# The causal convolution of a hybrid encoder layer as products with diagonal matrices, with v by token, a shorter reciprocal root and two x blocks transposed by TensorE

## The chip, the cores and the metric

One core of a Trainium2 chip runs the whole layer in one program. The metric is the time on the device in microseconds, lower is better. For the kernel before there are three timed runs and one profiled execution.

## The reference, cut to what matters

Two requests (x_prompt and x_sample, 2048 tokens of 1024 features each, in float32) go through one encoder layer with the same weights. The change concerns group B, the gated DeltaNet branch.

```python
def encoder_layer(x, mem, ...):
    hx = rms_norm(x, pre_g)
    proj = hx @ w_in
    a_u, a_z, b_qkv, b_z, b_gates, c_qkv, c_z, d_q, d_z = jnp.split(proj, IN_SPLITS, axis=-1)
    y_a = fourier_mix(a_u, w_fnet) * jax.nn.silu(a_z)
    y_b = gdn_branch(b_qkv, b_gates, conv_w, ...) * jax.nn.silu(b_z)
    ...
    out = jnp.concatenate([y_a, y_b, y_c, y_d], axis=-1) @ w_out
    return x + rms_norm(out, post_g)

def gdn_branch(qkv, gates, conv_w, ...):
    act = jax.nn.silu(centred_dwconv(qkv, conv_w)).astype(jnp.float32)
    q, k, v = jnp.split(act, 3, axis=-1)
    q = l2_norm(q.reshape(b, l, h, HEAD_DIM)) * (HEAD_DIM ** -0.5)
    k = l2_norm(k.reshape(b, l, h, HEAD_DIM))
    ...
    o_f = gdn_chunked(q, k, v, g[:, :, 0], beta[:, :, 0])
    o_b = rev(gdn_chunked(rev(q), rev(k), rev(v), ...))
```

centred_dwconv is a convolution over five tokens of each of 768 channels by itself (256 of q, k and v, in 4 heads of 64); gdn_chunked works in chunks of 64 tokens, each of which first needs k, q and v of its tokens, then an inverse of a triangular matrix, and then the state of the chunk before.

## The kernel before, in words

Numbers of float32 precision are made from f16 products: each operand is split into a high and a low f16 half, and a product is three products (lines 484 to 486 with token blocks as the right operand, 494 to 496 with them as the left, 500 to 502 elsewhere). A scheduler orders the instructions of each engine once, at build time, by priorities of the parts ("bands") and its own estimates; on the chip each engine then runs its list in that order. So an instruction that waits holds up all behind it on its engine, and a transfer is issued when its queue (SP's, or ACT's for stores of projections) comes to it.

The program, in the order of its data:

- pass_a, for each request 8 blocks of 256 tokens. xblock (lines 448 to 470) normalises a block, splits it (ACT L466 high, DVE L213 low) and lets SP's DMA transpose it (L468) to features by tokens; block() stores it for later sweeps (xTd). For each block the units k, q, v and ag (a_u and the gates) are projected on TensorE (feat, pj, L484 to L486), evacuated by ACT (L561) into st, and stored by ACT's queue into braw, in HBM, f32, with two tokens of padding at either end (L518, L519). For the very first block the weights of each unit are loaded and split just ahead (L385, L415, L419, L421; L431 takes the maxima that set a scale).
- The convolution, conv_pair (L880 on), for each block and each of k, q, v. It loads 260 tokens of two 128-channel groups from braw (craw, L885) and sums five taps by channel: ACT the first (L889), DVE the other four (L891, one instruction of 128x256 for each tap and group), then tanh on ACT (L893) and the product that makes the SiLU on DVE (L894). ACT and POOL split the result into f16 halves (L901, L227: kq for k and q, vt for v). v is then transposed by a DMA on SP (L960) from channels by tokens to tokens by channels, vr, and stored for the chain. Squares of k and q are summed over a head on PE (pss, L909), and norms() makes reciprocal roots of them.
- gdn_pair, for each two chunks: kbd on DVE, the products of k with k and q (PE L500 to L502 into p12, in the PSUM tags ga and gq in turn), and DVE's products with the decay mask (L1013). The last of these ends what is called the preparation here. gdn_sub (from L1056) inverts the triangular matrices, gdn_chain (L1133) runs the states in order, 32 steps each way for both requests.
- Beside and behind them, as fillers by priority: the Fourier part (fnet), memory and neighbourhood attention, the second sweep (pass_b, projections for the attention groups), the third (pass_z, gate paths) and the output projection (pass_o).

rsqrt (L232 to L245) computes a reciprocal root on DVE: a first guess by integer shift and subtraction (L239, L240), and three Newton steps of three instructions (L243 to L245).

## Time and profile before

| | us |
|---|---|
| median of three runs | 2527.11 (2523.99 to 2535.14) |
| the profiled execution | 2518.5 |
| its span | 2516.7 |
| busy in the span: PE, DVE, POOL, ACT | 2006.7, 2013.1, 1128.9, 1034.4 |
| first projection on PE starts | 64.4 |
| last evacuation of pass_a (L568) starts | 653.9 |
| last mask product of the preparation (L1013) starts | 892.9 |
| state chain (L1133), first and last start | 1485.8, 2111.7 |

The profile's times are of one execution; its span leaves out 1.8 us around it. PE is TensorE, PEld its weight loads (which run beside products), DVE VectorE, ACT ScalarE, POOL GpSimd, SP the engine that issues most transfers. Busy time is the union of the instructions of an engine. PEclk is the granted share of TensorE's full clock.

### The profile page before, as it was taken

Reading aid. Unit: us, or ns where it says so; the run is one execution under the profiler, and the core shown is the slowest. Engines: PE = TensorE matmul, PEld = TensorE weight load, DVE = VectorE, ACT = ScalarE, POOL = GpSimd, SP = SyncE. Lnnn points to the kernel's source line nnn. Section 1 sums busy time; section 2 is a strip of 40 time slices with the busy share of each in tenths; the row PEclk is TensorE's granted clock in tenths of the full one; section 3 lists DMA queues with packets and bytes.
Section 4 is the critical chain, followed back from the end, with each engine's and each line's share of the span. In section 5 each row is a group of like instructions: output and inputs, shape, how many; then the busy total and the mean of one; then the engine's idle time right before and its main releaser. Section 6 shows DMA issues by size and latency. Waiting matters only on the chain. (4 is left out here: it accounts for less than half of the span.)

```text
span 2516.7 us, 60042 instructions
## 1 busy us (share of the span) xinstructions
PE 2006.7 (80%) x23715; PEld 1701.4 (68%) x23715; DVE 2013.1 (80%) x4757; ACT 1034.4 (41%) x2434; POOL 1128.9 (45%) x1181
## 2 busy tenths in 40 slices
PE   0787778787446786899698988887788899899998
PEld 0665667665335675777576767777677788688887
DVE  3579988989999979668989667887679977677774
ACT  1455554553354421334056423554445523332322
POOL 1225655445476667535786152232234343533220
PEclk9988899998768988999799999999999999899999
DMA  9899899999635694599789877999999995555543
GB/s 94 193 210 178 200 232 239 233 209 234 180 94 159 168 222 118 142 218 179 153 187 200 181 195 210 229 199 210 198 214 224 217 279 164 169 182 187 187 161 118
DMA packets 827484, 476.08 MB, mean 189 GB/s; under 512 B 556864, under 2 KB 789952, under 8 KB 818752
## 3 DMA queue, kind: packets, MB, share of 16 engines
q1 hardware_dynamic: 802624, 438.67, 76.0%
q10 hardware_dynamic: 24576, 33.56, 4.5%
q8 instruction: 186, 3.05, 0.5%
q14 instruction: 98, 0.80, 0.1%
HBM read 243.38 MB, written 163.73 MB: 162 GB/s over the span
## 5 line engine op out<-in xcount | busy, mean ns | idle before, releaser
L484 PE MATMUL pj<-xT,w 128*128 128x256 f16 x2592 | 741.1, 286 | 119.7 <-DMA xT<-xh 35.7
L486 PE MATMUL pj<-xT,w 128*128 128x256 f16 x2592 | 739.5, 285 | 4.0 <-POOL w L421 4.0
L485 PE MATMUL pj<-xT,w 128*128 128x256 f16 x2592 | 740.6, 286 | 0.0
L485 PEld LDWEIGHTS <-w 128*128 128x128 f16 x2592 | 265.1, 102 | 109.4 <-issue 67.7
L484 PEld LDWEIGHTS <-w 128*128 128x128 f16 x2592 | 265.1, 102 | 102.7 <-issue 31.4
L486 PEld LDWEIGHTS <-w 128*128 128x128 f16 x2592 | 265.3, 102 | 52.8 <-POOL w L421 9.4
L502 PE MATMUL po<-w,oy 128*128 128x256 f16 x1024 | 280.3, 274 | 1.4 <-DVE oy L716 1.4
L500 PE MATMUL po<-w,oy 128*128 128x256 f16 x1024 | 280.7, 274 | 0.8 <-ACT oy L715 0.8
L501 PE MATMUL po<-w,oy 128*128 128x256 f16 x1024 | 280.9, 274 | 0.0
L891 DVE SCALAR_TENSOR_TENSOR cacc<-craw,cws,cacc 128x256 f32<-128x256 f32 x384 | 244.4, 671 | 7.4 <-ACT cacc L889 6.2
L494 PE MATMUL pj<-w,xT 128*128 128x272 f16 (+1 forms) x512 | 153.3, 300 | 43.8 <-ACT st L561 21.8
L230 POOL TENSOR_TENSOR oy<-oy,oz 128x512 f32<-128x512 f32 x60 | 101.0, 1704 | 187.7 <-ACT oy L701 179.4
L1165 POOL COPY bk<-rA 64x512 f16<-64x512 f16 x124 | 85.8, 692 | 208.9 <-PE pw L502 171.2
L765 ACT ACTIVATE oj<-po,wsc_o 128x256 f32<-128x256 f32 x128 | 59.5, 469 | 243.9 <-PE po L502 243.1
L495 PE MATMUL pj<-w,xT 128*128 128x272 f16 (+1 forms) x512 | 153.0, 299 | 0.8 <-POOL w L421 0.8
L496 PE MATMUL pj<-w,xT 128*128 128x272 f16 (+1 forms) x512 | 152.9, 299 | 0.0
L421 POOL TENSOR_TENSOR w<-wt,w 128x512 f16<-128x512 f32 (+1 forms) x70 | 85.1, 1223 | 145.9 <-ACT w L419 118.4
L227 POOL TENSOR_TENSOR mP<-mP,mP 128x1024 f16<-128x1024 f32 x32 | 71.6, 2241 | 137.0 <-DVE ty L1503 52.9
L500 PE MATMUL pno<-nPT,nv 128*128 128x64 f16 x704 | 78.5, 199 | 57.9 <-DMA nPT<-np__2819_27983 20.2
L1170 DVE COPY b<-rA 64x1536 f16<-64x1536 f16 x128 | 112.4, 878 | 8.1 <-DMA cT<-T 3.7
L227 POOL TENSOR_TENSOR km<-kt,km 128x256 f16<-128x256 f32 x128 | 96.4, 775 | 38.0 <-ACT km L1009 36.2
L1485 ACT ACTIVATE mP<-pms,ty,mds 128x256 f32<-128x256 f32 x128 | 71.0, 560 | 97.7 <-DVE ty L1482 76.0
(442 smaller groups left out, 6162.7 us busy)
## 6 DMA issues: line engine op xcount, KB each, us to landing
xT<-xTd SPq DMA_DIRECT2D x32, 1024.0 KB
rec<-km SPq DMA_DIRECT2D x32, 768.0 KB
rA<-rec SPq DMA_DIRECT2D x64, 384.0 KB
xTd<-xT SPq DMA_DIRECT2D x16, 1024.0 KB
sz<-st ACTq DMA_DIRECT2D x64, 256.0 KB
oz<-sz SPq DMA_DIRECT2D x16, 1024.0 KB
out_dram<-oo SPq DMA_DIRECT2D x32, 512.0 KB
craw<-braw SPq DMA_DIRECT2D x48, 260.0 KB
```

Source lines behind the costliest of these rows:

```text
L227: self.nc.gpsimd.tensor_tensor(out=out, in0=a, in1=b, op=ALU.subtract)
L484: nc.tensor.matmul(ps, whi, xhi, start=(kt == 0), stop=False)
L485: nc.tensor.matmul(ps, whi, xlo, start=False, stop=False)
L486: nc.tensor.matmul(ps, wlo, xhi, start=False, stop=(kt == KT - 1))
L494: nc.tensor.matmul(ps, xhi, whi, start=(kt == 0), stop=False)
L495: nc.tensor.matmul(ps, xhi, wlo, start=False, stop=False)
L496: nc.tensor.matmul(ps, xlo, whi, start=False, stop=(kt == KT - 1))
L500: nc.tensor.matmul(ps, whi, xhi, start=start, stop=False)
L501: nc.tensor.matmul(ps, whi, xlo, start=False, stop=False)
L502: nc.tensor.matmul(ps, wlo, xhi, start=False, stop=stop)
L891: nc.vector.scalar_tensor_tensor(out=acc[:, f], in0=raw[:, f, t:t + CB], scalar=w[:, t:t + 1], in1=acc[:, f], op0=ALU.mult, op1=ALU.add)
L1170: nc.vector.tensor_copy(b1[s, :, h].rearrange("p (d x) c -> p d x c", d=2), ra[s, :, 0:12])
```

## The change

- The convolution becomes products on TensorE. conv_diag makes, once, a table cdg of diagonal matrices 64x64 for each unit, channel group, head and tap, as f16 high and low halves (three pieces, each two DVE instructions and one of ACT over 1280 elements, and a small one for the scale). braw is kept as f16 high and low halves: ACT evacuates the high half, DVE's split_lo the low one (from PSUM, 128x512), and only then ACT's queue stores both. craw holds for one head the high half of 64 channels on partitions 0 to 63 and the low half on 64 to 127; four loads of 64 partitions bring it where there was one, and it has four buffers instead of two. Ten products (five taps, two table halves) add up in PSUM (pcv, in the tags ga and gq) for each group and head: 64 output rows by 256 columns for q and k (L935), with the two heads in turn. tanh and the SiLU product (now L939) read PSUM.
- v's products (L929) have the tokens as weights and the table as right operand, 64 by 64 each, with the two groups in turn, so they come out by token: vr is written at once, and the DMA transposes L960 go.
- The low half of q and v is now DVE's (split_lo, L214), k's stays with POOL. Scales move into the table and back by powers of two (CSH, cinp).
- rsqrt takes 8 instructions: one for the guess, one Newton step of three, and one step of higher order of four.
- xblock has a switch: the first two blocks of the first request are transposed by PE (64 transposes of 128x128) with eight ACT evacuations of 128x1024, in place of four DMA transposes.

```diff
     def rsqrt(self, x, out, eng=None):
...
-        nc.vector.tensor_scalar(out=y.bitcast(I32), in0=x.bitcast(I32), scalar1=1, scalar2=None, op0=ALU.logical_shift_right)
-        nc.vector.tensor_scalar(out=y.bitcast(I32), in0=y.bitcast(I32), scalar1=-1.0, scalar2=float(0x5F3759DF),
-                                op0=ALU.mult, op1=ALU.add)
-        for i in range(3):
-            eng.scalar_tensor_tensor(out=t, in0=y, scalar=-0.5, in1=y, op0=ALU.mult, op1=ALU.mult)
-            eng.scalar_tensor_tensor(out=t, in0=t, scalar=1.0, in1=x, op0=ALU.mult, op1=ALU.mult)
-            eng.scalar_tensor_tensor(out=(out if i == 2 else y), in0=t, scalar=1.5, in1=y, op0=ALU.add, op1=ALU.mult)
+        stt = lambda o, a, s, b, op: eng.scalar_tensor_tensor(out=o, in0=a, scalar=s, in1=b, op0=op, op1=ALU.mult)
+        nc.vector.tensor_scalar(out=y.bitcast(I32), in0=x.bitcast(I32), scalar1=-0.5, scalar2=float(0x5F3759DF), op0=ALU.mult, op1=ALU.add)
+        stt(t, y, -0.5, y, ALU.mult)
+        stt(t, t, 1.0, x, ALU.mult)
+        stt(y, t, 1.5, y, ALU.add)
...
+        c = math.sqrt(0.375)
+        stt(t, y, c, y, ALU.mult)
+        stt(t, t, 1.0, x, ALU.mult)
+        stt(t, t, -1.25 / c, t, ALU.add)
+        stt(out, t, 1.875, y, ALU.add)
...
-    def xblock(self, rows):
+    def xblock(self, rows, pe=False):
...
-            nc.sync.dma_start(dst[:, :, :, t * P:t * P + P].rearrange("p l k t -> p (l k) t"), hl.rearrange("p l c -> p (l c)"), transpose=True)
+            if pe:
+                for l in range(2):
+                    pt = self.pat.tile([P, KT, P], F16, name=self.nm("pxt"), tag=PSS[l])
+                    for k in range(KT):
+                        nc.tensor.transpose(pt[:, k], hl[:, l, k * P:k * P + P], self.ident16)
+                    nc.scalar.activation(dst[:, l, :, t * P:t * P + P], pt, AF.Copy)
+            else:
...
-            xT = self.xblock(x[tb * 256:tb * 256 + 256, :])
+            xT = self.xblock(x[tb * 256:tb * 256 + 256, :], pe=r == 0 and tb < 2)
...
-                nc.scalar.activation(st, ps, AF.Copy, scale=2.0 ** -19)
-                nc.scalar.dma_start(D[f"braw{r}"][:, f0:f0 + 2, 2 + tb * 256:258 + tb * 256], st)
+                st = self.stage([P, 2, 2, 256], F16)
+                nc.scalar.activation(st[:, :, 0], ps, AF.Copy, scale=2.0 ** -19)
+                self.split_lo(nc.vector, st[:, :, 1], ps, st[:, :, 0], 2.0 ** -19)
+                nc.scalar.dma_start(D[f"braw{r}"][:, f0:f0 + 2, :, 2 + tb * 256:258 + tb * 256], st)
...
+    def conv_diag(self, pp):
...
+        cg = self.cdg = pp.tile([P, 3, 20, 2, 64], F16, name="cdg", tag="cdg")
+        for i, u in ((1, "k"), (0, "q"), (2, "v")):
...
+            d = pp.tile([P, 20, 64], F32, name=self.nm("cdf"), tag="cdf")
+            nc.vector.tensor_tensor(out=d, in0=self.i2.unsqueeze(1).to_broadcast([P, 20, 64]), in1=w.unsqueeze(2).to_broadcast([P, 20, 64]), op=ALU.mult)
+            nc.scalar.activation(cg[:, i, :, 0], d, AF.Copy)
+            nc.vector.tensor_tensor(out=cg[:, i, :, 1], in0=d, in1=cg[:, i, :, 0], op=ALU.subtract)
...
     def conv_pair(self, r, pp, tb, u):
...
-        raw = pp.tile([P, 2, CB + 4], F32, name=self.nm("craw"), tag="craw", bufs=2)
-        nc.sync.dma_start(raw, self.D[f"braw{r}"][:, 2 * i:2 * i + 2, tb * CB:tb * CB + CB + 4])
...
-        for f in range(2):
-            w = self.cws[:, 2 * i + f]
-            nc.scalar.activation(acc[:, f], raw[:, f, 0:CB], AF.Copy, scale=w[:, 0:1])
-            for t in range(1, 5):
-                nc.vector.scalar_tensor_tensor(out=acc[:, f], in0=raw[:, f, t:t + CB], scalar=w[:, t:t + 1], in1=acc[:, f], op0=ALU.mult, op1=ALU.add)
...
-        nc.vector.scalar_tensor_tensor(out=acc, in0=e, scalar=1.0, in1=acc, op0=ALU.add, op1=ALU.mult)
+        raw = pp.tile([P, 2, 2, CB + 4], F16, name=self.nm("craw"), tag="craw", bufs=4)
+        src = self.D[f"braw{r}"].rearrange("(h e) a l t -> l h e a t", h=2)
+        for l in range(2):
+            for h in range(2):
+                nc.sync.dma_start(raw[64 * l:64 * l + 64, :, h], src[l, h, :, 2 * i:2 * i + 2, tb * CB:tb * CB + CB + 4])
+        pv = self.pgd.tile([P, 2 * CB], F32, name=self.nm("pcv"), tag="ga" if u == "q" else "gq")
+        dg = lambda f, h, t, l: self.cdg[:, i, (f * 2 + h) * 5 + t, l]
+        S = [(t, l) for t in range(5) for l in range(2)]
...
         if u == "v":
...
+            for n in range(CB // 64):
+                for h in range(2):
+                    for k, (t, l) in enumerate(S):
+                        for f in range(2):
+                            nc.tensor.matmul(pv[half(f), n * P + 64 * h:n * P + 64 * h + 64], raw[:, f, h, n * 64 + t:n * 64 + t + 64], dg(f, h, t, l),
+                                             start=(k == 0), stop=(k == 9))
         else:
+            for f in range(2):
+                for k, (t, l) in enumerate(S):
+                    for h in range(2):
+                        nc.tensor.matmul(pv[half(h), f * CB:f * CB + CB], dg(f, h, t, l), raw[:, f, h, t:t + CB], start=(k == 0), stop=(k == 9))
...
+        nc.scalar.activation(e, pv, AF.Tanh, scale=self.cinp[:, i:i + 1])
+        nc.vector.scalar_tensor_tensor(out=acc, in0=e, scalar=1.0, in1=pv, op0=ALU.add, op1=ALU.mult)
...
+            if u == "k":
+                self.gsub(dst[1], ac, dst[0])
+            else:
+                for f in range(2):
+                    self.split_lo(nc.vector, dst[1][:, f], ac[:, f], dst[0][:, f], sc)
...
-        self.nc.sync.dma_start(vr.rearrange("p n (x c) -> p (n x) c", c=P), self.vt.rearrange("p n l f c -> p (n l f c)"), transpose=True)
```

The order that the scheduler gives is another one throughout. Two places show it. The first is SP's list at the start, from the first padding stores of braw on (xt is a block of x on its way in, xT the transposed block, w the weights; w_277 and w_315 are q's, w_369 and w_408 v's). Before:

```order
L518 DMA braw_209<-ty_210 768x1x2
L519 DMA braw_209<-ty_210 768x1x2
L385 DMA w_277<-in_w_in_dram 128x8x256
L385 DMA w_369<-in_w_in_dram 128x8x64 x3
L456 DMA xt_654<-in_x_prompt_dram 128x1024
L518 DMA braw_3153<-ty_3154 768x1x2
L519 DMA braw_3153<-ty_3154 768x1x2
L468 DMA_TRANSPOSE xT_107<-xh_133 128x16x128
L468 DMA_TRANSPOSE xT_107<-xh_137 128x16x128
L385 DMA w_369<-in_w_in_dram 128x8x64
L385 DMA w_464<-in_w_in_dram 128x8x256
```

Now:

```order
L533 DMA braw_246<-ty_247 1536x1x2 x2
L392 DMA w_315<-in_w_in_dram 128x8x256
L392 DMA w_408<-in_w_in_dram 128x8x64 x3
L463 DMA xt_691<-in_x_prompt_dram 128x1024
L533 DMA braw_3219<-ty_3220 1536x1x2 x2
L463 DMA xt_695<-in_x_prompt_dram 128x1024
L463 DMA xt_1099<-in_x_prompt_dram 128x1024
L392 DMA w_408<-in_w_in_dram 128x8x64
L392 DMA w_504<-in_w_in_dram 128x8x256
```

The two transposes ahead of v's last piece of weights are gone, loads of x blocks stand there instead, and the padding is 1536 rows at a time.

The second is DVE's list in the middle of the convolution (gates, gw, gam, beta and ke belong to the gates of the chain, nrm to the norms, xh to the next x block). Before:

```order
L894 SCALAR_TENSOR_TENSOR cacc_13113<-cexp_13124,cacc_13113 128x512
L569 TENSOR_SCALAR gates_215<-pj_1461,wsc_ag 128x16
L213 SCALAR_TENSOR_TENSOR xh_1905<-xt_1881,ty_1890,xh_1905 128x1024
L213 SCALAR_TENSOR_TENSOR xh_1909<-xt_1885,ty_1890,xh_1909 128x1024
L891 SCALAR_TENSOR_TENSOR cacc_13283<-craw_13281,cws,cacc_13283 128x256 x2
L918 COPY nrm_13133<-pss_13042 64x8 x4
L891 SCALAR_TENSOR_TENSOR cacc_13283<-craw_13281,cws,cacc_13283 128x256
L569 TENSOR_SCALAR gates_215<-pj_1488,wsc_ag 128x16
```

Now:

```order
L214 SCALAR_TENSOR_TENSOR xh_2294<-xt_2273,ty_2278,xh_2294 128x1024
L224 TENSOR_TENSOR gw_1623<-gw_1623 128x32
L939 SCALAR_TENSOR_TENSOR cacc_13852<-cexp_13851,pcv_13810 128x512
L849 TENSOR_SCALAR beta_976<-gw_1619 128x4x8
L214 SCALAR_TENSOR_TENSOR st_1788<-pj_1739,st_1788 128x2x256
L858 COPY gam_979<-pga_1622 128x4x8
L865 TENSOR_SCALAR ke_978<-ke_978 128x4x8
L467 TENSOR_SCALAR ty_2413<-ty_2413 128x2
```

The runs of L891 are gone; between one L939 and the next stand the gates' work and a split of a projection, st, that was not there before.

## Rows read from the trace of the kernel before

**Rows 1.** Windows: stretch and length, busy us (instructions) by engine, then clock and DMA.
```profile
core 0: us, PE busy (x) PEld busy (x) DVE busy (x) ACT busy (x) POOL busy (x), PEclk, DMA share, GB/s
...
130.00:660.00 530.00, 410.82 (x3754) 341.05 (x3755) 485.90 (x1241) 251.50 (x556) 275.41 (x291) 0.88 0.99 218
660.00:890.00 230.00, 136.47 (x1259) 110.90 (x1257) 221.19 (x529) 107.42 (x243) 150.97 (x161) 0.77 0.53 142
890.00:1500.00 610.00, 511.55 (x5286) 414.20 (x5284) 495.61 (x898) 224.77 (x520) 353.28 (x369) 0.92 0.82 177
1500.00:2110.00 610.00, 507.81 (x9545) 452.91 (x9544) 482.34 (x1316) 281.99 (x709) 206.23 (x255) 0.96 0.94 217
2110.00:2517.00 407.00, 387.04 (x3488) 341.36 (x3486) 272.03 (x566) 127.29 (x334) 116.81 (x76) 0.98 0.48 168
0.00:890.00 890.00, 600.35 (x5403) 492.96 (x5404) 763.16 (x1978) 400.39 (x872) 452.62 (x481) 0.87 0.87 188
```

**Rows 2.** Line L1013: instructions, minimum/median/maximum ns, first and last start.
```profile
L1013 DVE TENSOR_TENSOR mt<-p,df x64: 401/414/419, 211.4 to 892.9; 128x256 f32<-128x256 f32 x64
```

**Rows 3.** Waits: who, for whom; us in total, times, longest.
```profile
ACT cexp L893 <- DVE cacc L891: 84.3, 27, 6.6
...
PE p L500 <- DVE mt L1013: 41.3, 25, 4.2
...
PE pj L484 <- DVE st L213: 32.6, 9, 6.7
...
ACT cacc L889 <- DMA craw<-braw: 16.8, 9, 3.5
```

**Rows 4.** Groups by form on DVE, the costliest: count, busy us, mean ns.
```profile
L891 DVE SCALAR_TENSOR_TENSOR cacc<-craw,cws,cacc 128x256 f32<-128x256 f32 x384 | 244.4, 671 | 7.4 <-ACT cacc L889 6.2
```

**Rows 5.** Groups by form on DVE: the reciprocal root's first step.
```profile
L243 DVE SCALAR_TENSOR_TENSOR ty<-ty 128x2 f32<-128x2 f32 x99 | 26.8, 271 | 2.4
```

**Rows 6.** Groups by form on DVE: the tanh product, a split from PSUM.
```profile
L894 DVE SCALAR_TENSOR_TENSOR cacc<-cexp,cacc 128x512 f32<-128x512 f32 x48 | 34.8, 724 | 2.2 <-ACT cexp L893 2.0
...
L213 DVE SCALAR_TENSOR_TENSOR st<-pj,st 128x512 f16<-128x512 f32 x32 | 21.9, 683 | 13.2 <-ACT st L619 13.1
```

**Rows 7.** Timeline of PE: start, length; products of 64 and of 256 columns.
```profile
1604.22 0.19 PE L500 MATMUL pno<-nPT,nv 128*128 128x64 f16 x1
1604.25 0.19 PE L501 MATMUL pno<-nPT,nv 128*128 128x64 f16 x1
...
2300.49 0.27 PE L500 MATMUL po<-w,oy 128*128 128x256 f16 x1
2300.60 0.27 PE L501 MATMUL po<-w,oy 128*128 128x256 f16 x1
```

**Rows 8.** Window inside the neighbourhood scores, columns as in rows 1.
```profile
1616.45:1617.23 0.78, 0.78 (x26) 0.78 (x24) 0.10 (x2) 0.78 (x3) 0.59 (x1) 1.00 0.66 146
```

**Rows 9.** Groups by form on PE in that window.
```profile
L502 PE MATMUL pns<-nkr,nqb 128*64 128x184 f16 x4 | 0.8, 246 | 0.0
L502 PE MATMUL pns<-nkr,nqb 128*64 128x69 f16 x4 | 0.8, 203 | 0.0
```

**Rows 10.** Timeline of all engines up to 65 us: start, length, instruction.
```profile
38.93 0.68 DVE L421 TENSOR_TENSOR w<-wt,w 128x512 f16<-128x512 f32 x1
...
48.30 1.13 ACT L419 ACTIVATE w<-wt 128x512 f16<-128x512 f32 x2
...
64.36 0.37 PE L484 MATMUL pj<-xT,w 128*128 128x256 f16 x1 [23.27 <-DMA xT<-xh]
...
64.74 0.42 PE L486 MATMUL pj<-xT,w 128*128 128x256 f16 x1
```

**Rows 11.** Groups by form on ACT and POOL.
```profile
L466 ACT ACTIVATE xh<-xt,ty 128x1024 f16<-128x1024 f32 x36 | 39.4, 1144 | 43.1 <-DVE ty L463 43.1
...
L227 POOL TENSOR_TENSOR kq<-cacc,kq 128x512 f16<-128x512 f32 x32 | 40.3, 1259 | 87.3 <-ACT kq L901 84.1 <-PE pdf L502 3.1
```

**Rows 12.** Groups by form of weight loads.
```profile
L484 PEld LDWEIGHTS <-w 128*128 128x128 f16 x2592 | 265.1, 102 | 102.7 <-issue 31.4 <-ACT w L419 11.1 <-DMA xT<-xh 8.6
```

More of the change, by code (lines that the diff above doesn't have):

```diff
@@ L273, in consts2 @@
         nc.gpsimd.tensor_copy(self.tri, st)
+        self.convg = self.ct([P, 60], F32, "convg")
+        nc.sync.dma_start(self.convg, I["convg"])
         st = self.stage([P, P], F32)
@@ L303, in conv_consts @@
             self.pow2_scale(m[:, i:i + 1], k, self.csc[:, i], 18 - k)
-            for f in range(2):
-                nc.vector.tensor_scalar(out=self.cws[:, 2 * i + f], in0=self.convw[:, 2 * i + f], scalar1=self.csc[:, i, 0:1],
-                                        scalar2=None, op0=ALU.mult)
             nc.vector.tensor_tensor(out=self.cinv[:, i:i + 1], in0=self.csc[:, i, 1:2], in1=self.wsc[u][:, 1:2], op=ALU.mult)
+            nc.vector.tensor_scalar(out=self.cinp[:, i:i + 1], in0=self.cinv[:, i:i + 1], scalar1=2.0 ** self.CSH[u], scalar2=None, op0=ALU.mult)
         s = self.tt([P, 3], tag="cvs")
@@ L514, in pass_a_alloc @@
         nc = self.nc
-        br = self.dt([P, 6, 2052], F32, f"braw{r}")
-        zt = self.tt([P, 6, 2], tag="zpad")
+        br = self.dt([P, 6, 2, 2052], F16, f"braw{r}")
+        zt = self.tt([P, 12, 2], F16, tag="zpad")
         nc.vector.memset(zt, 0.0)
-        nc.sync.dma_start(br[:, :, 0:2], zt)
-        nc.sync.dma_start(br[:, :, 2050:2052], zt)
+        for o in (0, 2050):
+            nc.sync.dma_start(br.rearrange("p a l t -> p (a l) t")[:, :, o:o + 2], zt)
         self.dt([P, 16, 256], F32, f"au{r}")
@@ L556, in body @@
                 self.wnext()
-            st = self.stage([P, 2, 256], F32)
             if u != "ag":
@@ L560, in body @@
                 ps = self.feat(W[u], xT)
[L561 to L562 removed]
+                st = self.stage([P, 2, 2, 256], F16)
+                nc.scalar.activation(st[:, :, 0], ps, AF.Copy, scale=2.0 ** -19)
+                self.split_lo(nc.vector, st[:, :, 1], ps, st[:, :, 0], 2.0 ** -19)
+                nc.scalar.dma_start(D[f"braw{r}"][:, f0:f0 + 2, :, 2 + tb * 256:258 + tb * 256], st)
                 return
+            st = self.stage([P, 2, 256], F32)
             d = self.wsc["ag"][:, 1:2]
@@ L878, in gdn_gates2 @@
             self.unit_rows(pp, x, self.dt([2, NCH, 2, P], F32, f"{nme}{r}"))
+    def conv_diag(self, pp):
+        nc = self.nc
+        cg = self.cdg = pp.tile([P, 3, 20, 2, 64], F16, name="cdg", tag="cdg")
+        for i, u in ((1, "k"), (0, "q"), (2, "v")):
+            w = self.tt([P, 20], tag="cvw")
+            nc.vector.tensor_scalar(out=w, in0=self.convg[:, 20 * i:20 * i + 20], scalar1=self.csc[:, i, 0:1], scalar2=2.0 ** -self.CSH[u],
+                                    op0=ALU.mult, op1=ALU.mult)
+            d = pp.tile([P, 20, 64], F32, name=self.nm("cdf"), tag="cdf")
+            nc.vector.tensor_tensor(out=d, in0=self.i2.unsqueeze(1).to_broadcast([P, 20, 64]), in1=w.unsqueeze(2).to_broadcast([P, 20, 64]), op=ALU.mult)
+            nc.scalar.activation(cg[:, i, :, 0], d, AF.Copy)
+            nc.vector.tensor_tensor(out=cg[:, i, :, 1], in0=d, in1=cg[:, i, :, 0], op=ALU.subtract)
     def conv_pair(self, r, pp, tb, u):
@@ new lines, in conv_pair @@
+        e = pp.tile([P, 2 * CB], F32, name=self.nm("cexp"), tag="cexp", bufs=2)
+        acc = pp.tile([P, 2 * CB], F32, name=self.nm("cacc"), tag="cacc", bufs=2)
+        nc.scalar.activation(e, pv, AF.Tanh, scale=self.cinp[:, i:i + 1])
+        nc.vector.scalar_tensor_tensor(out=acc, in0=e, scalar=1.0, in1=pv, op0=ALU.add, op1=ALU.mult)
+        sc = 2.0 ** self.CSH[u]
+        if u == "v":
+            ac = acc.rearrange("p (n c) -> p n c", c=P)
+            nc.scalar.activation(self.vr[:, :, 0], ac, AF.Copy, scale=sc)
+            self.split_lo(nc.vector, self.vr[:, :, 1], ac, self.vr[:, :, 0], sc)
+        else:
+            ac = acc.rearrange("p (f n c) -> p f n c", f=2, c=64)
@@ L908, in conv_pair @@
                     for k in range(3):
-                        nc.tensor.matmul(self.pss[:, t, 2 * i + f], ep[k][:, f, t * P:t * P + P], self.onesbd[:, 0:P:64], start=(k == 0), stop=(k == 2))
+                        nc.tensor.matmul(self.pss[:, t, 2 * i + f], ep[k][:, f * CB + t * P:f * CB + t * P + P], self.onesbd[:, 0:P:64], start=(k == 0), stop=(k == 2))
     def norms(self, r, pp, tb):
```

29 lines of the change are left out of this document (13 added, 16 removed).

## The prediction

> **What bounds the kernel now.** I read first the windows of the trace, since shares over the whole span mix stages with different limits. In [rows 1] the reader is to see that the stretch from 130 to 660 us, where the convolution runs between the projections, is VectorE's: DVE is busy 486 of 530 us (92%), TensorE 411 (78%, at a granted clock of 0.88); and so are the 230 us after the last projection, with DVE at 221 (96%) and PE at 136. From 890 us on PE is the busier engine or near it (512 of 610, 508 of 610, 387 of 407). The last mask product of the chunk preparation, which ends the first part, starts at 892.9 us [rows 2]; what follows in the program (inverse, state chain) needs it. So the question is what the first 890 us become, and what later stages take over.
>
> Second, the waits: PE and ACT stand there for DVE [rows 3]. ACT's tanh waited 84.3 us, 27 times, for the accumulation L891, and PE's score product 41.3 us, 25 times, for DVE's mask product. Third, the groups on DVE: L891, 384 instructions and 244.4 us, is the largest [rows 4], a third of DVE's 763 us up to 890.
>
> **What the change takes from DVE up to 890 us.** L891, which the order shows between gates, norms and mask products, goes: -244. The reciprocal root has 8 instructions for 11; three of the kind of [rows 5], 271 ns, are 0.81 us; 59 calls make 48 us in the program, of which 34 calls (18 of x blocks and memory, 16 of the norms), 28 us, lie in this part. **What it adds there:** 48 splits of the projections from PSUM, 128x512, by the 683 ns of the same form in [rows 6]: +33. 32 splits of q's low half, 128x256: no such row; between 414 and 671 ns [rows 2, 4], I take 600 as both inputs come from SBUF, as L891's do: +19 (13 to 21). 16 of v's, 128x512, by L894's 724 ns [rows 6]: +12. Six table instructions of 1280 elements, by L894's time for 512, 1.8 each: +11. Together 763 - 272 + 75 = 566 us. Busy at 92% from 40 us on (below), DVE alone would let this part end near 655 us.
>
> **What it adds to PE.** 1280 products of 256 columns with 64 output rows for k and q, and 2560 of 64 columns for v. Full-clock spacing is 0.11 us for 256 columns and 0.03 (0.029) for 64, each with its own weights [rows 7]. One after the other: 1280 x 0.109 + 2560 x 0.029 = 140 + 74 = 214. The code issues the two halves of the output (h for k and q, f for v) in turn, so they may overlap. The only products with 64-column weights now, the neighbourhood scores, do: in 0.78 us there are 24 loads, and products of 184 and 69 columns in each of three lines, four of one and three or four of the other [rows 8, 9]; some 2900 columns, 1.23 us at the spacing above, so a ratio near 1.6. Full overlap would make it 107. I take 1.5 for k and q (93) and none for v (74), since no row shows a product start sooner than 0.029 after the last: **167**, bounds 107 and 214. The 64 transposes of 128 columns are about 4, mostly in time in which PE now stands.
>
> The new order also moves work out: up to the last preparation product PE has 276 products of the second sweep and 78 of the Fourier part fewer than before, 354 x 0.109 = 39 us. And the clock: 0.87 up to 890 where PE is idle in between, 0.92 to 0.98 in the stages where it is busier [rows 1]. I take 0.93 for a PE that now has more to do: 600 x 0.87 / 0.93 = 562; with no rise it stays at 600. PE's sum: 562 - 39 + 167 + 4 = **694** us, more than DVE's 566, so the bound changes engine.
>
> **The start.** PE's first projection begins at 64.36 us and waited 23.27 us for the two DMA transposes [rows 10]. In the new order SP has v's last weight loads there instead, and block 0's transposes stand at PE's head, but k's last low weight half comes at 38.93 + 0.68 on DVE, behind the maxima of q's weights, which wait for a load [rows 10]. That stays, so PE starts near 40, not earlier. Block 0's k is 96 products, of which two start within 0.38 us there [rows 10], some 18 us; q's weights, made from 48.30 on by ACT, come behind eight evacuations of the form of L466 (8 x 1.14 = 9 us) [rows 11], so near 60, in time. Gain here: 24, bounds 0 and 30.
>
> **The end of this part.** An engine that bounds is busy 92% (DVE, 130 to 660) to 95% (PE, last window) [rows 1]; I take 93%. 40 + 694 / 0.93 = 786 us instead of 893: **-107**.
>
> **Costed at nothing.** ACT loses the 96 copies before L891 and gains the 9 us; POOL loses 32 subtractions of 1.26 us [rows 11], 40; at 400 and 453 of the first 890 us [rows 1] neither sets the pace, and where one did it would be a gain. SP loses 16 transposes for v and issues four loads of 64 partitions where it had one; the wait for these was 16.8 us in 9 times [rows 3], and there are now four buffers instead of two; if they came late each time at that price, 1.9 us, PE would stand 48 x 1.9 = 90. An added wait: ACT issues the store of the projections, and now only after DVE's split; behind it on ACT stand the next evacuation and the tanh. ACT's 84 us of waits for L891 go, and I set the one against the other. The projection's bank also stays taken until that split; the same pattern in the second sweep made PE wait 32.6 us for 64 splits [rows 3], 0.5 each, so 0 to 24 us here.
>
> **What comes back later.** The 39 us, 16 of them in the stage from 890 to 1500, 10 beside the chain and 15 (139 products of the third sweep more) after it, where PE is 95% busy. The last is paid in full, the others nearly (PE at 84%): **+30**, bounds 0 and 45.
>
> Sum: 2518.5 - 107 + 30 = 2441. The profiled execution took 2518.5 us, 8.6 under the median of the three runs, 2527.1; on that footing 2450.
>
> **Rivals.** *B, the halves overlap fully and DVE and PE share the work well.* PE's sum is 634, this part ends at 40 + 634 / 0.93 = 722, the time is 2518.5 - 171 + 30 + 9 = 2386, and 2356 if the moved products find gaps. For it: the ratio of 1.6 with uneven widths. Against: 93% for PE while DVE needs 566.
>
> *C, banks in order.* The 48 new products' groups lie in the two PSUM tags of the score products, and PE takes its instructions in order: it stands until ACT's tanh and DVE's product have let a bank go. Priced by PE's present wait of this kind, 41.3 / 25 = 1.65 us [rows 3]: 48 x 1.65 = 79, end of the part 865, time 2529: no change. For it: those are the very banks that PE waits for now. Against: DVE, for which it waits, has 200 us less to do.
>
> *D, loads set the pace: slower.* If a load of 64 columns takes half of the 102 ns of one of 128 [rows 12], 51 ns, and doesn't hide behind the products of the other half, the 3840 loads come on top: 107 + 196 = 303 in place of 167, 146 us more at 93%, the part ends at 932 and the time is 2518.5 + 39 + 30 + 9 = 2596. It decides from 62 ns a product on (238 in all, end at 863, where the 30 eat the gain). Against: in [rows 8] 24 such loads take 0.78 us, 32 ns each, with products running. For: most of those products have up to 184 columns to hide a load behind, v's have 64.
>
> The Trainium skill speaks for D: the page "TensorEngine Tiling (Array Packing)", Restrictions and Gotchas, says that column tiling excludes Fast Weight Load, and "TensorE: Matmul & The Clock Gate", LDWEIGHTS, puts a load at columns / 1.2 ns. By these 64 columns are 53 ns, an estimate from the page, and 3840 of them 204 us, so the sum by the rule would be about 2600. The trace's 32 ns a load speaks against it.
>
> **Chances.** The forecast 0.66, B 0.15, C 0.11, D 0.08. A measurement of this kernel can tell 0.5%, 12.6 us, from no change. Faster: the forecast, B and a little of C, 0.82; within 0.5%: the rest of C, 0.10; slower: D, 0.08. The low end takes in B with the moved work partly hidden, 2350. The high end, 2520, takes in the forecast with no rise of the clock (+41) and the projections' banks (+24); it leaves out D, most of C and a little below, under 2 in 10.
>
> **What would show it.** Right: DVE's share up to the last preparation product falls to about 72% and PE's rises above 85%, with a clock over 0.9; the part ends at 750 to 820 us; the first projection starts near 40; the products L929 and L935 take 140 to 190 us in all; after the chain the third sweep has some 15 us more. Wrong: half-width products 60 ns apart or more (D); long waits of PE's convolution products for ACT's tanh or DVE's L939, or for the loads of the rows (C); DVE still over 88% while PE waits for it.

## The result, and the profile after

The changed kernel takes 2684.28 us (median of 4 runs, 2681.62 to 2702.43), the kernel before 2526.31 beside it: ratio 1.0634, 95% interval 1.058 to 1.0688. It is 158 us slower, where a gain to about 2450 was forecast; the time lies outside the range. The profiled execution has a span of 2679.8 us.

Busy time of the whole span, from the head of the page after the change:

```profile
PE 2161.8 (81%) x27619; PEld 1842.8 (69%) x27619; DVE 1808.3 (67%) x4298; ACT 1009.7 (38%) x2349; POOL 1083.4 (40%) x1149
```

DVE lost 205 us of work (2013.1 before), PE gained 155 (2006.7 before), and the span grew by 163. Outside its busy time PE has 518 us of the span, and had 510 before. The windows of the trace after, with the columns of [rows 1], and the mask product of [rows 2]:

```profile
core 0: us, PE busy (x) PEld busy (x) DVE busy (x) ACT busy (x) POOL busy (x), PEclk, DMA share, GB/s
...
400.00:660.00 260.00, 203.62 (x2669) 171.72 (x2667) 130.01 (x363) 94.00 (x191) 96.23 (x112) 0.89 0.86 174
660.00:800.00 140.00, 91.66 (x1246) 76.62 (x1244) 56.89 (x151) 40.01 (x88) 58.39 (x72) 0.86 0.70 136
...
2250.00:2680.00 430.00, 410.48 (x3731) 362.86 (x3728) 245.48 (x519) 131.77 (x341) 117.73 (x76) 0.98 0.47 164
```

```profile
0.00:1002.00 1002.00, 713.43 (x8962) 595.89 (x8963) 565.23 (x1577) 369.54 (x771) 396.07 (x450) 0.86 0.77 157
```

```profile
L1062 DVE TENSOR_TENSOR mt<-p,df x64: 404/414/420, 221.2 to 1001.5; 128x256 f32<-128x256 f32 x64
```

The part that was to get shorter got 109 us longer (892.9 before). DVE is no longer near its limit there: 50% in the window from 400 us, where it had 92% [rows 1]. But PE has not become the full engine of the forecast either: 78% and 65% in the first two windows, and 71% (713 of 1002) up to the end of the part. All engines stand a good share of the time. What follows the part takes 1678 us instead of 1624. The waits, PE's and SP's:

```profile
PE pcv L935 <- DMA craw<-braw: 81.2, 23, 14.2
...
PE pj L498 <- DVE st L214: 53.6, 14, 10.5
...
PE pcv L929 <- DMA craw<-braw: 20.7, 8, 6.1
```

```profile
SPq L918 <- DMA braw<-st: 158.8, 33, 13.0
```

PE's 41 us of waiting for the mask product [rows 3] have shrunk to 16 up to the end of the part, and 102 us for the rows of the convolution are new; SP waits 159 us (33 times) until a stored projection has landed, to load it again (31 us, 7 times, before).

The start, from the timeline of all engines:

```profile
43.27 0.39 PE L500 MATMUL pj<-xT,w 128*128 128x256 f16 x1 [17.27 <-DVE w L428]
...
52.23 1.06 ACT L465 ACTIVATE xq<-xt 128x1024 f32<-128x1024 f32 x1 [29.87 <-DMA xt<-in_x_prompt_dram]
...
72.61 0.17 DVE L467 TENSOR_SCALAR ty<-ty 128x2 f32<-128x2 f32 x1 [26.43 <-ACT xq L465]
...
85.27 0.42 PE L498 MATMUL pj<-xT,w 128*128 128x256 f16 x1
```

PE's first projection starts at 19.7 us, stops at 26 and goes on at 43. But DVE then stands 26 us for the squares of x block 1, whose rows land late, with the scale of q's weights behind that in its list, and q's products start at 85. The gates' unit of block 0 is first evacuated at 133.0 us; before it was at 96.8.

### The profile page after: what moved, and what is told of

Same layout as the page of the kernel before. It is cut to its first block, busy times and chain, and to the rows that moved or that the text cites. A ratio compares the mean times of both kernels' runs of the same rounds, so it can differ in the third digit from the quotient of the medians.

```text
span 2679.8 us, 67382 instructions
## 1 busy us (share of the span) xinstructions
PE 2161.8 (81%) x27619; PEld 1842.8 (69%) x27619; DVE 1808.3 (67%) x4298; ACT 1009.7 (38%) x2349; POOL 1083.4 (40%) x1149
## 5 line engine op out<-in xcount | busy, mean ns | idle before, releaser
L935 PE MATMUL pcv<-craw,cdg 128*64 128x256 f16 x1280 | 111.6, 332 | 101.5 <-DMA craw<-braw 81.2
L508 PE MATMUL pj<-w,xT 128*128 128x272 f16 (+1 forms) x512 | 149.3, 292 | 32.7 <-DVE st L214 12.9
L935 PEld LDWEIGHTS <-cdg 128*64 128x64 f16 x1280 | 88.8, 134 | 116.2 <-DMA craw<-braw 74.5
L509 PE MATMUL pj<-w,xT 128*128 128x272 f16 (+1 forms) x512 | 150.1, 293 | 0.7 <-POOL w L428 0.7
L510 PE MATMUL pj<-w,xT 128*128 128x272 f16 (+1 forms) x512 | 150.0, 293 | 0.0
L214 DVE SCALAR_TENSOR_TENSOR st<-pj,st 128x512 f16<-128x512 f32 (+1 forms) x112 | 76.8, 685 | 54.2 <-ACT st L575 29.5
```

What stands on the lines that cost most here:

```text
L508: nc.tensor.matmul(ps, xhi, whi, start=(kt == 0), stop=False)
L509: nc.tensor.matmul(ps, xhi, wlo, start=False, stop=False)
L510: nc.tensor.matmul(ps, xlo, whi, start=False, stop=(kt == KT - 1))
L935: nc.tensor.matmul(pv[half(h), f * CB:f * CB + CB], dg(f, h, t, l), raw[:, f, h, t:t + CB], start=(k == 0), stop=(k == 9))
```

## The experiments

All were run beside the kernel before on the same chip, whose median was 2527 to 2548 us from chip to chip; so the ratios are compared. "End" is the start of the last mask product; the last two columns are PE's busy time of the whole span and what is left of the span.

Two limits hold for all of it. The end and PE's times are of one execution each, on different chips: e6, with the same products as the kernel before, shows 22 us more of PE's busy time, so differences of that size mean nothing. And the scheduler makes new lists for every kernel, so that each run is its edit together with another order; no run held the order fixed. The small edits e6, e14 and e1 move the ratio by 0.2%, 0.6% and 1.4%, so a difference of about 1% between two runs can't be put down to the edit alone.

| run | ratio (95%) | end, us | PE busy | PE not busy |
|---|---|---|---|---|
| before | 1 | 892.9 | 2006.7 | 510 |
| the change | 1.0634 (1.058 to 1.0688) | 1001.5 | 2161.8 | 518 |
| e12 first tap only | 0.9803 (0.9766 to 0.9841) | 828.2 | 2005.6 | 480 |
| e13 dummy products | 1.0522 (1.0494 to 1.0551) | 960.4 | 2148.7 | 505 |
| e16 both | 1.0374 (1.0345 to 1.0403) | 913.9 | 2139.4 | 475 |
| e6 root alone | 1.0023 (1.0002 to 1.0045) | 900.9 | 2028.8 | 523 |
| e7 v alone | 1.0276 (1.0236 to 1.0317) | 923.3 | 2082.4 | 529 |
| e2 old convolution | 1.0155 (1.0129 to 1.0181) | 919.0 | 2029.2 | 553 |
| e5 half products | 1.0503 (1.0457 to 1.0548) | 988.2 | 2099.6 | 563 |
| e3 one load | 1.0519 (1.0489 to 1.055) | 979.9 | 2160.9 | 508 |
| e4 block 0's rows | 1.0638 (1.0604 to 1.0672) | 987.2 | 2154.3 | 542 |
| e9, e10 lag of one, two | 1.06, 1.0522 | 1045.5, 1045.4 | 2171.1, 2156.6 | 526, 523 |
| e11 POOL's queue | 1.0616 (1.058 to 1.0652) | 1082.3 | 2167.1 | 527 |
| e1 no PE transposes | 1.0775 (1.0736 to 1.0814) | 1048.2 | 2165.1 | 574 |
| e15, e14 block 0 only | 1.0603, 1.0058 | 993.7, 909.3 | 2163.3, 2018.3 | 519, 518 |

### What DVE's relief is worth, and what PE's products cost

**e12**: the kernel before without L891, so that the convolution is its first tap alone.

```diff
-            for t in range(1, 5):
+            for t in range(1, 1):
                 nc.vector.scalar_tensor_tensor(out=acc[:, f], ...)
```

> The kernel before with the first tap alone (ACT's copy): the 384 accumulations L891 are left out, 244 us of DVE's 763 up to the end of the preparation, with nothing put in their place on PE and no load changed; the outputs that depend on the convolution are of other values. The prediction's step (DVE bounds this part, and PE alone would need far less): the part ends 130 to 200 us sooner than before, ratio 0.93 to 0.955. Theory A (PE's work and waits set the pace, DVE is busy within them): DVE's idle time grows by some 200 us and the end moves by less than 50 us, ratio 0.98 to 1.01.

**e13**: the products of the change on constants, in the kernel before. They read no data of the kernel, but they use the banks of the score products, as the change does. **e16** is e13 with e12's edit.

```diff
+        pv = self.pgd.tile([P, 2 * CB], F32, name=self.nm("pdm"), tag="ga" if u == "q" else "gq")
...
+                            nc.tensor.matmul(pv[half(f2), n * P + 64 * h:n * P + 64 * h + 64], d16[:, 0:64], d16[:, 64:128], start=(k == 0), stop=(k == 9))
...
+                        nc.tensor.matmul(pv[half(h), f2 * CB:f2 * CB + CB], d16[:, 0:64], d16.unsqueeze(1).to_broadcast([P, 2, P]), start=(k == 0), stop=(k == 9))
```

> The kernel before with the products of the change added on PE, but on constants (pieces of the identity) into a bank that nobody reads, in the same tags, so with no input to wait for; DVE keeps its 384 accumulations, and nothing of the result changes. The prediction's picture (PE has 290 us of room while DVE bounds): the products fill gaps, the end of the part moves by under 40 us, ratio 1.00 to 1.02. Theory A (PE's work adds to a nearly fixed idle time): PE's busy time up to that end rises by 100 to 150 and the end by 70 to 140 us, ratio 1.03 to 1.055.

> e13 with DVE's accumulations left out as in e12: the changed kernel's load on PE and DVE without its new waits, loads, stores and start. Theory A: near the changed kernel, the end of the part 100 to 150 us after that of e12, ratio 1.03 to 1.055. If the changed kernel's loss is mainly its new waits for rows (96 us) and its start: within 50 us of e12, ratio 0.98 to 1.0.

The windows up to the end of the preparation, of e12, e13 and e16:

```profile
0.00:829.00 829.00, 580.42 (x5339) 482.78 (x5340) 571.72 (x1597) 395.89 (x871) 440.66 (x483) 0.90 0.95 202
```

```profile
0.00:961.00 961.00, 684.28 (x8759) 577.43 (x8759) 741.51 (x1943) 393.94 (x846) 454.08 (x482) 0.85 0.76 169
```

```profile
0.00:914.00 914.00, 666.69 (x8704) 565.74 (x8705) 541.58 (x1557) 389.64 (x845) 427.53 (x481) 0.86 0.80 177
```

The four kernels make a square of two causes:

| ratio | DVE accumulates | accumulations left out |
|---|---|---|
| no products added | 1 | 0.9803 |
| products added | 1.0522 | 1.0374 |

Leaving out 244 us of DVE's work shortens the kernel by 2.0% (50 us), and with the products there by 1.5% (37 us); the part ends only 65 us sooner. The products cost 5.2% (132 us) with DVE at work and 5.7% (145 us) without, although they wait for no data; e13's alone occupy PE for 152 us up to the end (a window for their tile pdm: PE's busy time, then clock and DMA), e16's for 141:

```profile
0.00:960.40 960.40, 152.14 (x3840) 0.85 0.76 169
```

Their price is not all paid in the part itself. What follows it, before and in e13:

```profile
892.90:2516.70 1623.80, 1403.50 (x18288) 1205.87 (x18286) 1248.29 (x2776) 632.93 (x1561) 675.11 (x698) 0.95 0.78 189
```

```profile
960.40:2653.50 1693.10, 1464.45 (x18797) 1262.09 (x18796) 1289.16 (x2817) 643.69 (x1588) 684.91 (x699) 0.94 0.77 186
```

The part ends 68 us later, and 509 products of other work, which ran within it before, come after it: another 69 us.

In e12 DVE is busy 69% and PE 70% up to the end, yet little is gained. The gain has one place. The last evacuation of the first sweep (pass_a, L568) starts at 657.4 us, where it was 653.9; from there to the last mask product (L1013) it takes 171 us instead of 239:

```profile
L568 ACT ACTIVATE st<-pj x32: 359/364/384, 106.2 to 657.4; 128x256 f32<-128x256 f32 x32
```

```profile
L1013 DVE TENSOR_TENSOR mt<-p,df x64: 402/412/418, 195.7 to 828.2; 128x256 f32<-128x256 f32 x64
```

In this last stretch of the kernel before DVE was busy 96% [rows 1], and 74 us of L891 fell there: with them left out it is 68 us shorter, though 34 of these come back behind the end (1658 us for 1624). The 170 us of L891 up to 660, most of it in the stretch with DVE at 92%, bought nothing. L891 in the kernel before (DVE's busy time, then clock and DMA):

```profile
0.00:660.00 660.00, 170.27 (x278) 0.90 0.99 204
660.00:893.00 233.00, 74.17 (x106) 0.77 0.53 145
```

This is the stretch from 130 to 660 us in e12, e13, e16 and the changed kernel (columns of [rows 1]):

```profile
130.00:660.00 530.00, 409.43 (x3823) 343.13 (x3823) 381.09 (x1048) 271.24 (x599) 294.66 (x317) 0.89 1.03 226
```

```profile
130.00:660.00 530.00, 402.82 (x5377) 343.62 (x5377) 436.75 (x1128) 240.30 (x521) 268.78 (x287) 0.88 0.80 187
```

```profile
130.00:660.00 530.00, 410.27 (x5522) 351.61 (x5519) 313.49 (x894) 245.31 (x536) 260.98 (x298) 0.90 0.84 191
```

```profile
130.00:660.00 530.00, 407.32 (x5334) 344.71 (x5333) 269.90 (x772) 199.16 (x417) 201.64 (x231) 0.88 0.82 166
```

PE is busy 76% to 77% in all four, and 78% before, whether DVE is at 92%, 72% or 51% (in e2, e4, e5 and e7 it is 73% to 75%). One rival stays for e12: the busy share of the DMA engines is given as 0.99 there before [rows 1] and as 1.03 in e12, so they may have held the sweep when DVE no longer did; no run tried that. It doesn't explain the other three, where the share is 0.80 to 0.84.

Theory A's ratios held in e13 and e16, and in e12 at their edge (0.98); its ends did not: 65 us in e12 where it said under 50, 68 later in e13 (70 to 140), with 81 us more of PE's work instead of 100 to 150, and 86 behind e12's in e16 (100 to 150). The prediction's own picture (0.93 to 0.955 for e12, 1.00 to 1.02 for e13) is refuted by both.

### Parts of the change by themselves

**e6**: rsqrt of the change in the kernel before. **e7**: v's products, table and split in the kernel before, k and q as they were. **e2**: the change with the old convolution. **e5**: the change with half of its products. The edits of e6 and e2 are the pieces rsqrt and xblock of the change's diff; those of e5 and e7:

```diff
-        S = [(t, l) for t in range(5) for l in range(2)]
+        S = [(t, 0) for t in range(5)]
...
```

```diff
-        for u in "kqv":
+        for u in "kq":
             self.conv_pair(r, pp, tb, u)
+        self.conv_v(r, pp, tb)
...
```

> The kernel before with the shorter reciprocal root alone. If DVE's work sets the time of the first part of the kernel before (as the prediction had it), 28 us of work less there end it 20 to 28 us sooner, and with the 20 us less in the later parts the ratio is 0.985 to 0.992. If the first part is paced by waits between the engines, the ratio is 0.997 to 1.003; and if another list order costs something, over 1.003, which then is a part of the 1.0155 of the old convolution with the root and the two x blocks.

> The kernel before with v's convolution alone on TensorE (2560 products by token, one table, no transposes of v); k and q as before, old reciprocal root, all x blocks by DMA. DVE loses 81 us of L891 and gains 22 + 12 + 4. Theory D (DVE bounds the first part while PE has room): the part ends 20 to 45 us sooner than before, ratio 0.98 to 0.992. Theory A (PE's products and idle add up): PE gets 60 to 75 us, the part ends 20 to 60 us later, ratio 1.01 to 1.03.

> The kernel before with the shorter reciprocal root and the two PE-transposed x blocks alone; the convolution as before on ACT and DVE. Theory C (the convolution on TensorE costs what is lost): the last mask product comes 10 to 28 us sooner than before (893), because 28 us of DVE work are gone where DVE bounds, and the time is 2495 to 2515. If theory S holds as well, the late start of 36 us eats that: 2520 to 2540. Rival (the convolution is not the cause): over 2600.

> The changed kernel with the high half of the diagonal table alone: five products for each sum instead of ten, so the convolution is less exact; loads, waits and all else the same. Theory A (up to the end of the preparation PE's products and PE's idle time simply add up: 713 us busy and 289 idle in the changed kernel, 603 and 290 before): some 83 us of PE's work go, the last mask product comes 60 to 85 us sooner than in the changed kernel, ratio to before 1.03 to 1.04. Theory R (the round trips through DRAM set the time of a block, whatever PE does): PE's idle grows by what its work falls, the end moves by less than 25 us, ratio 1.05 to 1.065.

The root alone is no gain. v alone loses 2.8%, with 76 us more of PE over the span: theory A's side. e2 was expected at 2495 to 2540 us and came out 1.5% slower than before (2565 beside the 2526 of the kernel before), with no product of the convolution on PE. None of its theories gave that; the end is 26 us later, and PE has 43 us more of not working, with 23 more of busy time, about as in e6.

e5 goes against theory A and came out as theory R said: the end is 13 us sooner than in the changed kernel (under 25; A had 60 to 85), the ratio 1.0503 (R 1.05 to 1.065, A 1.03 to 1.04). R's cause, the round trips through DRAM, finds no support in e4 below. What e5 shows is that PE's busy time falls by 62 us over the span and its other time grows by 45: taking work off PE gave back 1.3%, some 33 us, about half of it.

### The loads of the rows

**e3**: one load of 128 partitions, with braw laid out for it and the store in four pieces. **e4**: the rows of the first request's block 0 for all. **e11**: POOL's queue. **e9**, **e10**: a copy on POOL ahead of the loads that needs the gates of the next block (tb + 1 below), or of the one after (tb + 2).

```diff
-        for l in range(2):
-            for h in range(2):
-                nc.sync.dma_start(raw[64 * l:64 * l + 64, :, h], src[l, h, :, 2 * i:2 * i + 2, tb * CB:tb * CB + CB + 4])
...
+        nc.sync.dma_start(raw.rearrange("p h f t -> p (h f) t"), src[:, :, tb * CB:tb * CB + CB + 4])
...
```

```diff
-        src = self.D[f"braw{r}"].rearrange("(h e) a l t -> l h e a t", h=2)
+        src = self.D["braw0"].rearrange("(h e) a l t -> l h e a t", h=2)
...
-                nc.sync.dma_start(raw[64 * l:64 * l + 64, :, h], src[l, h, :, 2 * i:2 * i + 2, tb * CB:tb * CB + CB + 4])
+                nc.sync.dma_start(raw[64 * l:64 * l + 64, :, h], src[l, h, :, 2 * i:2 * i + 2, 0:CB + 4])
```

```diff
+                nc.gpsimd.dma_start(raw[64 * l:64 * l + 64, :, h], ...)
```

```diff
+        g = 2 * min(tb + 1, 7) + 1
+        nc.gpsimd.tensor_copy(raw[:, :, :, 0:1], self.gates[r][:, g, 0:4].rearrange("p (a b) -> p a b", a=2).unsqueeze(3))
```

> The changed kernel with one load of 128 partitions for each unit on SP instead of four of 64; the store of a projection is four pieces on ACT's queue instead of one. Theory Q (SP's list: 192 loads of 0.6 us each hold up all behind them): SP is free of some 85 us, the last mask product comes 40 to 80 us sooner than 1001, the time 2600 to 2640. Theory L (the loads wait for the landing of the next block's store, and PE stands for that round trip in its order): under 20 us gained, 2660 to 2690, and PE's wait for craw stays near 100 us.

> The changed kernel, but every load of the convolution takes the rows of the first request's first block, so that no load waits for a store just made; the same products, loads and stores otherwise, and the outputs that depend on the convolution are those of other data. Theory L (the round trip from the store of a projection to the load): SP's waits for braw (158.8 us) and PE's for craw (81 and 21 us) all but go, the last mask product comes 60 to 100 us sooner than 1001, the time 2580 to 2620. Theory Q (the number of SP's issues) or theory O (PE's work of 711 us in a part where products follow each other through four engines): less than 25 us sooner, PE's waits move to other lines.

> The changed kernel with the loads of the rows on POOL's queue in place of SP's, nothing else. Theory Q2 (SP's list stands for the landings of stores, 148 us, and holds up the loads of x, the transposes, the gates' rows behind it): SP waits little, the part ends 30 to 70 us sooner than in the changed kernel, ratio 1.035 to 1.05, though POOL's list then stands for those landings. If POOL's issues and waits hold up the splits that PE's score products need: 1.06 or more.

> The changed kernel with one small copy on POOL ahead of the four loads of each unit, which takes the gates of the next block as input, so that the loads of a block's rows come only after the next block's last projection (its stores have landed by then, or nearly); the products and all else the same. Theory O (PE, SP stand because the lists put the convolution right behind the store it depends on): SP's waits for braw (148 us from 165 us on) fall under 60, PE's for craw (96) under 50, the part ends 30 to 70 us sooner than in the changed kernel, ratio 1.035 to 1.05. Theory A (PE's idle time, some 290 us up to the end of this part in each of the kernels, stays whatever it waits for): ratio 1.055 to 1.075.

> As e9_lag_one, with the gates of the block after the next. Theory O: no waits for craw or braw of note, and the end as in e9 or up to 20 us sooner. If the convolution then comes too late for what follows it, the end is later than in e9. Theory A: as e9, other waits in their place.

In e4 the waits for the rows all but went, and these are what PE and SP waited for instead (165 us to the end):

```profile
PE p L514 <- DVE mt L1062: 67.3, 13, 19.8
...
PE pcv L935 <- DMA craw<-braw: 11.0, 4, 7.2
```

```profile
SPq L1030 <- DMA gamd<-gT: 63.6, 6, 21.1
```

The ratio stayed at 1.0638, with the end 14 us sooner. So the longest wait of the profile after, the round trip of the projections through DRAM, was not what held the time: theory L falls, and its numbers for e4 (2580 to 2620) are missed by far.

The other runs gain little or nothing. In e3 PE still waits 101 us for the rows and the end is 22 us sooner, near what L gave (under 20) and far from Q; the ratio is 1.0519. In e9 SP's waits for braw fall to 25 us and PE's for craw to 66, and the ratio is 1.06, in theory A's range. In e10 they are 19 and 49 us and the ratio is 1.0522, but with an end 44 us later than in the changed kernel, because more of the second sweep comes ahead of it (some 440 more projection products by the end). POOL's queue (e11) gives nothing, with an end 81 us later.

**e8** was a miss: k's projections, and q's of the first request, copied straight into rows in SBUF.

```diff
...
+                        nc.scalar.dma_start(self.rawt[r, f0 // 2][64 * l:64 * l + 64, h, :, 2 + tb * 256:258 + tb * 256], st[64 * h:64 * h + 64, :, l])
...
```

> The changed kernel with k's projections of both requests and q's of the first copied straight from the evacuation's tile into an SBUF row buffer that the convolution reads (four pieces on ACT's queue), without the way through DRAM and without SP's loads (96 left of 192). Theory L (the round trip by DRAM and SP holds PE up): PE's wait for craw falls under 40 us, the part ends 40 to 70 us sooner than in the changed kernel, ratio 1.035 to 1.05. Theory A (waits only move to the next thing in PE's list): as with block 0's rows for all, other waits take their place, ratio 1.055 to 1.07.

The ratio was 1.1991. The first mask product came at 554 us instead of 221: presumably the rows in SBUF leave no room for the preparation beside the first sweep, which wasn't tried out. It says nothing of the round trip.

### The start

**e1**: all x blocks by DMA. **e15**: the second of the two too. **e14**: the first x block by PE, in the kernel before.

```diff
-            xT = self.xblock(x[tb * 256:tb * 256 + 256, :], pe=r == 0 and tb < 2)
+            xT = self.xblock(x[tb * 256:tb * 256 + 256, :], pe=False)
```

```diff
+            xT = self.xblock(x[tb * 256:tb * 256 + 256, :], pe=r == 0 and tb < 1)
```

> The changed kernel with one part undone: all x blocks are transposed by DMA again. In the changed kernel the first evacuation of the gates' unit (L584) starts at 133.0 us, 36 us later than before (96.8), since q's first products start at 85 us. Theory S (the PE transposes put DVE's and ACT's work for block 1 ahead of q's weights and so delay the start): L584 starts near 97 to 105 us and the time falls by 25 to 36 us, to 2650 to 2660. Rival (the start is absorbed later, or the load of v's weights and the doubled pads delay it): L584 stays above 120, the time within 10 us of 2684.

> The changed kernel with the first x block alone transposed by PE. If block 1 is what delays the start: the first gates' unit comes near 110 instead of 142, ratio 1.05. Otherwise as the changed kernel, 1.06, or as without any (1.0775).

> The kernel before with the first x block alone transposed by PE. The first projection starts near 20 and, after k's last weight half, goes on near 44 us. If block 1's norm in DVE's list ahead of q's weights is what delays the start where two blocks go this way: the gates' first unit comes 10 to 25 us sooner than with two (124.5) and no later than with none (108 on this chip), ratio 0.985 to 1.0. Otherwise (the lists change anyway): ratio 1.0 to 1.015.

Theory S is not borne out: without PE transposes the changed kernel is slower still (1.0775; the gates' unit is first evacuated at 125 us, so over 120 as the rival had it, but the time isn't the changed kernel's either). With the first block alone it is evacuated at 123 us in e15 and at 115 in e14, and little changes (1.0603, 1.0058). In e12, e13 and e16, whose edits leave the start alone, it is at 102 to 106 where it was 96.8 before, so not all of the 36 us needs a cause in the change. What delays the start in each of these lists wasn't followed up.

## Why the prediction was wrong

**The counts were right, with some luck.** DVE's work up to the end was forecast at 566 us and is 565. PE's was forecast at 694 and is 713. The 3840 new products occupy it for 177 us where 167 were forecast, 46 ns each (a window for their tile pcv: busy time of PE, DVE and ACT, then clock and DMA):

```profile
0.00:1000.00 1000.00, 176.99 (x3840) 32.75 (x48) 32.71 (x48) 0.85 0.77 157
```

Here two errors partly cancel. For k and q full-clock spacing divided by 1.5 gave 93 us and it is 112; for v, with no overlap, 74 and it is 66 (by form, up to the end):

```profile
L935 PE MATMUL pcv<-craw,cdg 128*64 128x256 f16 x1280 | 111.6, 332 | 101.5 <-DMA craw<-braw 81.2 <-DVE mt L1062 12.2 <-DMA L<-lt 8.1
```

```profile
L929 PE MATMUL pcv<-cdg,craw 128*64 128x64 f16 x2560 | 65.7, 212 | 31.8 <-DMA craw<-braw 20.7 <-issue 9.2 <-DVE cacc L939 1.9
```

The new groups on DVE came out as priced (684 ns for 683, 660 for 600, 784 for 724):

```profile
L214 DVE SCALAR_TENSOR_TENSOR st<-pj,st 128x512 f16<-128x512 f32 x80 | 54.7, 684 | 44.4 <-ACT st L575 29.5 <-ACT st L635 14.4
L939 DVE SCALAR_TENSOR_TENSOR cacc<-cexp,pcv 128x512 f32<-128x512 f32 x48 | 32.8, 684 | 102.0 <-ACT cexp L938 101.9
...
L214 DVE SCALAR_TENSOR_TENSOR kq<-cacc,kq 128x256 f16<-128x256 f32 x32 | 20.0, 660 | 10.5 <-ACT kq L949 9.8 <-issue 0.7
...
L214 DVE SCALAR_TENSOR_TENSOR vr<-cacc,vr 128x512 f16<-128x512 f32 x16 | 12.6, 784 | 2.1 <-ACT vr L943 1.9
```

**The step that failed** is "An engine that bounds is busy 92% to 95%; I take 93%": it turned PE's 694 us into an end at 786. PE was busy 71% (713 of 1002). The rows said 92% of DVE and I read from it that PE's 290 us without work up to 890 were room. They were not. With 244 us of DVE's work taken out and nothing added, PE still stands 249 of 829 us (e12); with the products added it stands 277 of 961 (e13). The reading that DVE bounds fits the stretch behind the first sweep, where DVE was at 96% and its relief shortened it by 68 us. It was wrong for the sweep itself, where DVE was at 92%: there PE is at 76% to 78% whatever DVE does.

PE's list is fixed, and PE stands in it for many short waits on the other engines, 290 us in all up to the end before and 289 in the changed kernel; in e4, when the longest kind was taken away, others were there. Over the whole span PE is without work for 475 to 574 us in all of the table's kernels (786 in e8), so added work lands on top: 155 us more of PE work are 163 us of span. That what is left over stays about the same is what the runs show; why it does is argued here from the waits, and e5, where it grew by 45 us as 62 of work went, shows that it is no constant.

**The clock** was to rise to 0.93, as PE would work more. The granted clock is 0.86 up to the end (0.87 before). With no rise the forecast's own terms give 600 - 39 + 177 + 4 = 742 us, and 713 were measured; where the 29 us went wasn't followed up.

**The start** was to gain 24 us. PE began at 19.7, earlier than told, and the stop for the low half of k's weights came as told (43.27 for "near 40"). That q's weights would be there near 60 was wrong: DVE's list has the norm of x block 1 ahead of them. The gates' unit is 36 us later, but the runs on the start above don't show that the whole of it counts.

**Costed at nothing.** The loads of the rows do hold PE up, 102 us, more than the 90 named as their price if they came late, where 0 was taken. But taking the wait away gains nothing by itself (e4). What the change loses beyond e16, which has the same relief and the same products and no new wait, load or start, is 2.6%, some 66 us. Candidates are the loads, the 75 us of new DVE work, the start, the longer time of the products (177 us for 141) and the order of the lists. The loads and the start, taken out alone, gave between 1.4% of loss and 1.2% of gain; the others weren't taken out, and how the 2.6% divides stays open.

**What comes back later** was 30 and is 54 us (1678 for 1624), above its bound of 45.

**The rivals.** D was the only one on the slow side, and for a wrong reason. The loads of weights take longer than those of 128 columns [rows 12], 125 ns in the mean, but overlap one another and the products:

```profile
L929 PEld LDWEIGHTS <-craw 128*64 128x64 f16 x2560 | 57.2, 125 | 37.7 <-issue 29.2 <-DMA craw<-braw 6.4 <-DMA L<-lt 0.2
```

At 46 ns a product, loads included, they lie under the 62 ns from which D decided. The rule cited for it from the Trainium skill ("TensorE: Matmul & The Clock Gate", LDWEIGHTS: 53 ns for 64 columns, an estimate from the page) isn't the pace here either. C named the kind (PE in order, standing for something new), but the convolution's products wait for the mask product for only 12 us, 2 times, and for L939 for 2; of its signs only the wait for the rows came, and that wait is not what cost the time (e4). The case that came true, that PE's share stays at some 70% and added products are paid nearly in full, was among neither the rivals nor the bounds, though [rows 1] held it: PE at 84% and 83% also in the two windows from 890 to 2110 us, where it is the busiest engine.

## What to carry to other kernels

A stage in which one engine is busy 92% is not shown to be bound by it: leave its work out in one run (here one line), and see stretch by stretch what the time does, before that work is moved to another engine. Here 170 us of it in a stretch at 92% bought nothing, 74 us in the next, at 96%, went with 68 us of time, of which 34 came back later, and the whole kernel gained 50. Where an engine runs a fixed list through short waits on all the others, take its busy share as it is, also for the work that is added: at 70 to 80% busy, PE paid 0.87 us of time for each us of products that waited for no data (132 for 152 in e13), and 1.03 in e16 (145 for 141). Work taken off it came back at about half (33 for 62 in e5).

## What the runs showed of the hardware

Products with 64 output rows in turns on the two halves overlap: 3840 of them, two thirds 64 columns and one third 256 wide, take 177 us with the table, and with constants as weights and data 152 (e13, up to the end) and 141 (e16); one after the other, at the full-clock spacing of [rows 7], they would be 214. That the constants take 14% to 21% less at a granted clock of 0.85 to 0.86 throughout was not expected and not followed up.
